# A hybrid retention/SSD layer on eight cores: x's third chunk moved ahead of two weight slabs, a norm weight folded into w_out, fewer LayerNorm statistics, more work on GpSimd, warm-up matmuls, and a new instruction order

## The chip, the cores and the metric

The kernel runs on all 8 cores of one Trainium2 chip. Each core works on its own requests with the same weights. There is no traffic between cores. The time of a run is that of its slowest core, in device microseconds.

Engines: PE is TensorE (matmul), DVE is VectorE, ACT is ScalarE, POOL is GpSimd, SP is the engine that issues part of the DMAs.

## The reference, cut to what matters

```python
def adaln(cond, w_ada, b_ada):
    return jax.nn.silu(cond) @ w_ada + b_ada            # 12 slabs of w_ada in the kernel

def trunk_layer(x, mod, rope, s_ret0, s_ssd0, p):
    sh1, sc1, g1, sh2, sc2, g2 = jnp.split(mod, 6, axis=-1)
    h = x * (1 + sc1) + sh1
    proj = h @ p['w_in']                                # q k v g (retention, 4 heads), z x B C dt (SSD)
    ...                                                 # bidirectional retention and SSD scans
    o_ssd = rms_norm(y * silu(z)) * p['ssd_norm_w']
    mix = jnp.concatenate([o_ret, o_ssd], axis=-1) @ p['w_out']
    x = layer_norm(ALPHA * x + g1 * mix, p['ln1_g'], p['ln1_b'])
    h2 = x * (1 + sc2) + sh2
    ffn = (silu(h2 @ p['w_gate']) * (h2 @ p['w_up'])) @ p['w_down']
    return layer_norm(ALPHA * x + g2 * ffn, p['ln2_g'], p['ln2_b']), ...
```

Per core there are 1536 tokens in three chunks of 512. Chunk 2 is context (group A). Chunks 0 and 1 are latent (group B).

## The kernel before

The kernel records operations and orders them itself when it is built: a list scheduler simulates the engines with a cost table and fixes one instruction order for each engine. Each engine then runs its list strictly in that order. Loads have an assumed duration in that table:

```python
            if o.is_dma:
                s0 = max(srv[0], st + 1.3)
                srv[0] = s0 + o.nbytes / (290e3 if e == POOL else 320e3)
                o.fin = srv[0] + 1.2          # the same for every core
# ... emit:
        self.schedule({})                     # first order, to learn lifetimes
        ...
            extra = self.place(slack)         # SBUF addresses; reuse gives extra dependencies
        order = self.schedule(extra)          # final order
```

Priorities (a lower level goes first), the order of stages and the triggers of loads are parameters. An entry such as `xr1="b2"` lets the rows of x for group A be fetched when the projections of latent head 2 are done.

```python
LV = dict(ht=0.9, conv=1.1, tm=1.1, prep=1, ssdA=0.8, ssdB=1, ..., headA=2, headB=1.7, evA=0.9, evB=0, outA=1.6,
          outB=1.5, evoA=0.7, evoB=0, ada=1.2)
SEQ = ("ssdA", "headA", "ssdB", "ada", "headB", "outA", "outB")
LD = dict(..., a6="p0A", a8="z7", h13="a1", a7="b0", a9="b0", ..., xr1="b2", xr0="b3", gate01="a3", ...)
```

A slab of weights is 128 x 4096 float32 in HBM and lands as bfloat16, by a DMA from the POOL queue. The start, and three places that the change touches:

```python
    w_in[1] = slab_load("w_in1", w_in_d[1], 4096, after=[xTo[(2, 1)]])
    ada[0] = slab_load("ada0", w_ada_d[0], 4096, after=[xTo[(2, 1)]])   # shift vector, first half
    ada[1] = slab_load("ada1", w_ada_d[1], 4096, after=[xTo[(2, 1)]])
    for q in range(2):                                                  # x, third chunk
        xTo[(1, q)] = P.dma(POOL, xT[(1, q)], xT_d[1, :, ...], after=[xTo[(2, 1)]])
    # ...
    def ssd_prep(g):                       # dt, decay: a chain of small ops on DVE and ACT
        ts(UU, AX, 1.0, ALU.add); act(LL, UU, AF.Ln); ...; tt(AX, AX, LL, ALU.mult); ...
    # ... end of ssd_block: norm weight applied while PSUM is evicted
        tt(oT[t // 4][:, :, o_:o_ + 128], ps..., nwc..., ALU.mult)
    # ... LayerNorm after the out-projection
        tt(dst[:, hs], bank, gate[:, hs], ALU.mult)
        stt(dst[:, hs], xres[:, hs], ALPHA, dst[:, hs], ALU.mult, ALU.add, accum_out=col(s, 16 * i))
        act(junk[:, hs], dst[:, hs], AF.Square, accum_out=col(s, 16 * i + 8))
```

## Time and profile before

| | before |
|---|---|
| time, median of 4 runs | 736.64 us (735.62 to 737.09) |
| span of the profiled slowest core | 733.4 us |
| PE busy / DVE / ACT / POOL | 91 / 56 / 42 / 32% |
| start of the block of 1516 matmuls (FFN and down projection) that nothing interrupts | 403.41 us |

From the page of the profile, before: the span, the busy times, and the two rows that show PE and its granted clock in 40 equal slices of the span (tenths).

```profile
span 733.4 us, 13130 instructions; the slowest of 8 cores (722.6 to 733.4 us)
PE 664.6 (91%) x4186; PEld 346.7 (47%) x4186; DVE 411.7 (56%) x896; ACT 309.1 (42%) x546; POOL 236.9 (32%) x277
PE   0598999999969989945999999999999999999995
PEclk9898999999999999976999999999999999999998
```

PE is idle in the first slices and dips around slices 18 and 19, where its clock falls too. From about 348 us on it is full. The longest waits of PE on this core (who waited for whom, us in total, times, longest):

```profile
PE psum L632 <- ACT arena L657: 22.5, 7, 16.2
PE psum L632 <- DVE arena L690: 11.1, 1, 11.1
PE psum L632 <- DMA arena<-w_ada: 5.7, 2, 4.9
PE psum L632 <- DMA arena<-w_in: 1.6, 1, 1.6
```

The first is mostly the start, which the change keeps. The 11.1 us wait is the seam: LayerNorm A is late and the FFN cannot begin. The same core by stretches: window, its length, then busy us (and instructions) of PE, PE weight load, DVE, ACT and POOL, then granted clock, DMA share and GB/s.

```profile
55.00:110.00 55.00, 51.44 (x460) 31.66 (x459) 30.56 (x90) 45.91 (x72) 17.55 (x56) 0.94 0.85 170
110.00:165.00 55.00, 53.95 (x359) 28.72 (x357) 43.04 (x82) 46.64 (x76) 36.20 (x45) 1.00 0.30 68
165.00:257.00 92.00, 82.24 (x711) 49.15 (x710) 75.15 (x123) 49.04 (x79) 49.18 (x56) 0.98 0.67 120
257.00:348.00 91.00, 69.35 (x600) 45.27 (x598) 68.58 (x139) 47.89 (x78) 51.45 (x50) 0.87 0.54 111
```

Window minus PE busy is PE's idle time: 3.6, 1.1, 9.8 and 21.7 us.

### The profile page before, as it was taken

The numbers are of one execution on the slowest core, as the hardware profiler recorded it, in microseconds if no ns is written. First come the engines' busy times: TensorE is split into PE (matmuls) and PEld (weight loads), VectorE is DVE, ScalarE is ACT, GpSimd is POOL, SyncE is SP. The second block draws the span as 40 slices with busy tenths as digits, with TensorE's granted clock in tenths as the row PEclk, the third lists the DMA queues.
The fourth block names the chain that finished last, engine by engine and source line by source line (L and its number), as shares of the span: only waits on it lengthen the run. The fifth ranks groups of instructions, "written<-read, shape, count | busy, mean of one in ns | idle before, by whom it ended". The sixth has DMA issues, their size and how long they took to land.

```text
span 733.4 us, 13130 instructions; the slowest of 8 cores (722.6 to 733.4 us)
## 1 busy us (share of the span) xinstructions
PE 664.6 (91%) x4186; PEld 346.7 (47%) x4186; DVE 411.7 (56%) x896; ACT 309.1 (42%) x546; POOL 236.9 (32%) x277
## 2 busy tenths in 40 slices
PE   0598999999969989945999999999999999999995
PEld 0255654556544656624446444444444444444443
DVE  5746275899867968877687212122112112486666
ACT  2657898877662445537556211111111111222221
POOL 3104042896454567543120169940000000000000
PEclk9898999999999999976999999999999999999998
DMA  8999951068982489430135433326292002022111
GB/s 249 332 171 240 173 96 46 21 137 151 161 153 52 87 138 177 126 109 1 58 102 130 115 57 58 59 44 124 49 171 44 1 30 86 1 87 87 57 58 58
DMA packets 14643, 75.08 MB, mean 102 GB/s; under 512 B 2656, under 2 KB 3040, under 8 KB 7920
## 3 DMA queue, kind: packets, MB, share of 16 engines
q0 software_dynamic: 5616, 42.47, 32.3%
q1 hardware_dynamic: 8960, 31.77, 12.9%
q8 instruction: 35, 0.57, 0.3%
q14 instruction: 32, 0.26, 0.1%
HBM read 106.05 MB, written 8.40 MB: 156 GB/s over the span
## 4 chain that ended last, share of the span: by engine, by line
PE 78%; DMA 10%; issue 4%; DVE 4%; ACT 2%; POOL 2%; SPq 1%; DVEq 0%; ACTq 0%; POOLq 0%
PE psum L632 76%; DMA arena<-w_in 5%; DMA arena<-w_ada 4%; DVE arena L682 2%; PE psum L635 2%; DVE arena L696 1%; POOL arena L682 1%; ACT arena L657 1%; ACT L657 1%; SPq L192 1%; DVE arena L690 0%; POOL arena L192 0%; POOL arena L707 0%; DVE arena L717 0%; DVE arena L720 0%
## 5 line engine op out<-in xcount | busy, mean ns | idle before, releaser
L632 PE MATMUL psum<-arena 128*128 128x512 bf16 (+5 forms) x4078 | 652.7, 319 | 60.5 <-ACT arena L657 22.5
L632 PEld LDWEIGHTS psum<-arena 128*128 128x128 bf16 x4078 | 333.6, 99 | 374.8 <-issue 86.9
L682 POOL TENSOR_TENSOR arena<-arena 128x512 f32<-128x512 f32 (+5 forms) x160 | 197.1, 1249 | 138.9 <-ACT arena L657 39.2
L657 ACT ACTIVATE arena<-psum 128x512 bf16<-128x512 f32 (+2 forms) x184 | 104.6, 579 | 243.1 <-PE psum L632 209.9
L682 DVE TENSOR_TENSOR arena<-arena,psum 128x512 bf16<-128x512 bf16 (+3 forms) x134 | 86.7, 653 | 180.9 <-PE psum L632 175.9
L657 ACT ACTIVATE arena<-arena 128x512 bf16<-128x512 f32 (+7 forms) x200 | 113.5, 588 | 145.4 <-DVE arena L696 92.7
L682 DVE TENSOR_TENSOR arena<-psum,arena 128x512 f32<-128x512 f32 (+6 forms) x187 | 116.6, 643 | 42.7 <-PE psum L632 37.1
L696 DVE SCALAR_TENSOR_TENSOR arena<-arena 128x512 f32<-128x512 f32 (+1 forms) x99 | 71.0, 752 | 4.3 <-DVE arena L682 2.3
L657 ACT ACT_TABLE_LOAD x43 | 55.2, 1283 | 19.2 <-PE psum L632 9.7
L657 ACT ACTIVATE arena<-psum,arena 128x512 bf16<-128x512 f32 (+2 forms) x58 | 36.1, 648 | 12.2 <-PE psum L632 6.9
L690 DVE TENSOR_SCALAR arena<-arena 128x1 f32<-128x1 f32 (+2 forms) x112 | 23.1, 216 | 31.1 <-ACT arena L657 21.6
L707 DVE CAST arena<-psum 128x512 bf16<-128x512 f32 (+2 forms) x42 | 25.2, 605 | 14.3 <-PE psum L632 10.7
L682 DVE TENSOR_TENSOR arena<-arena 128x8 f32<-128x8 f32 (+8 forms) x55 | 22.3, 412 | 4.6 <-PE psum L632 3.2
L707 POOL CAST arena<-arena 128x2 bf16<-128x2 f32 (+1 forms) x51 | 13.0, 345 | 31.3 <-DVE arena L707 24.8
L707 DVE CAST arena<-arena 128x256 bf16<-128x256 f32 (+8 forms) x35 | 17.4, 500 | 8.6 <-DMA arena<-w_ada 5.1
L192 POOL DMA_DIRECT2D arena<-w_gu x11 | 6.3, 572 | 49.4 <-PE psum L632 28.6
L1289 DVE COPY_PREDICATED psum<-arena,psum 128x512 f32<-128x512 uint16 x24 | 16.6, 693 | 9.8 <-PE psum L632 9.5
L688 DVE TENSOR_SCALAR arena<-arena 128x128 bf16<-128x128 f32 (+5 forms) x78 | 17.1, 266 | 6.0 <-ACT arena L657 5.4
L635 PE MATMUL psum<-arena 128*128 128x128 f32 (+1 forms) x108 | 15.7, 291 | 0.8 <-DVE arena L717 0.6
L192 POOL DMA_DIRECT2D arena<-w_in x10 | 6.0, 604 | 29.8 <-DVE arena L688 26.1
L635 PEld LDWEIGHTS psum<-arena 128*128 128x128 f32 (+1 forms) x108 | 13.5, 150 | 4.2 <-issue 2.7
L720 DVE TENSOR_SCALAR arena<-arena 128x512 bf16<-128x512 f32 x24 | 11.4, 511 | 4.1 <-DMA arena<-xT 4.0
(20 smaller groups left out, 58.7 us busy)
## 6 DMA issues: line engine op xcount, KB each, us to landing
arena<-w_gu POOLq DMA_DIRECT2D x11, 1024.0 KB, 10.1
arena<-w_in POOLq DMA_DIRECT2D x10, 1024.0 KB, 13.5
arena<-w_ada POOLq DMA_DIRECT2D x10, 1024.0 KB, 17.5
arena<-x SPq DMA_DIRECT2D x12, 512.0 KB, 3.5
arena<-w_down POOLq DMA_DIRECT2D x4, 1408.0 KB, 16.5
y<-arena SPq DMA_DIRECT2D x11, 512.0 KB, 2.7
arena<-w_ada SPq DMA_DIRECT2D x4, 1024.0 KB, 15.8
arena<-xT SPq DMA_DIRECT2D x4, 1024.0 KB, 22.1
```

The source lines that it names most:

```text
L192: o = self.add({eng: (0.9 if eng == POOL else 0.45, lambda e: e.dma_start(out=R(out), in_=R(in_)))}, [in_], [out], after=after)
L632: return P.add({PE: (c, lambda e: e.matmul(R(out), lhsT=R(lhsT), rhs=R(rhs), start=start, stop=stop))}, [lhsT, rhs], [out])
L635: return P.add({PE: (0.12, lambda e: e.transpose(out=R(out), in_=R(in_), identity=R(ident_f)))}, [in_, ident_f], [out])
L657: fn = lambda e: e.activation(out=R(out), in_=R(in_), func=func, **{k: R(v) for k, v in kw.items()})
L682: fn = lambda e: e.tensor_tensor(out=R(out), in0=R(in0), in1=R(in1), op=op)
L688: fn = lambda e: e.tensor_scalar(out=R(out), in0=R(in0), scalar1=R(s1), scalar2=None, op0=op0)
L690: fn = lambda e: e.tensor_scalar(out=R(out), in0=R(in0), scalar1=R(s1), scalar2=R(s2), op0=op0, op1=op1)
L696: fn = lambda e: e.scalar_tensor_tensor(out=R(out), in0=R(in0), scalar=R(scalar), in1=R(in1), op0=op0, op1=op1, **{k: R(v) for k, v in kw. ...
L707: alts[g] = (vcost(g, out, [in_], "copy"), lambda e: e.tensor_copy(out=R(out), in_=R(in_)))
L720: lambda e: e.tensor_scalar(out=R(out), in0=R(in_), scalar1=R(scale), scalar2=R(bias), op0=ALU.mult, op1=ALU.add))
L1289: P.add({DVE: (0.7, lambda e, eb=eb, ef=ef, mk_=mk_: e.copy_predicated(R(eb), R(mk_), R(ef)))}, [mk_, ef, eb], [eb])
```

## The change

Intent: fill PE's idle stretches and take small work off DVE. The diff, cut to its core:

```diff
+WARM = 8
-LV = dict(ht=0.9, conv=1.1, tm=1.1, prep=1, ssdA=0.8, ssdB=1, ... evA=0.9, evB=0, outA=1.6, outB=1.5, evoA=0.7, evoB=0, ada=1.2)
+LV = dict(ht=1.1, conv=1.1, tm=1, prep=1.1, ssdA=0.8, ssdB=0.8, ... evA=0, evB=0, outA=1.6, outB=1.5, evoA=1.25, wo=1.2, evoB=0.7, ada=1.7)
-OPT = dict(rope="q")
+OPT = dict(rope="qk", swap="")                # k's rotary swap by ACT and POOL too
+ENG = dict(wo="V", pr="P", ht="AVP", ...)     # SSD prep on POOL; modulation of x on ACT, DVE or POOL
-SEQ = ("ssdA", "headA", "ssdB", "ada", "headB", "outA", "outB")
+SEQ = ("ssdA", "headA", "ada", "ssdB", "outA", "headB", "outB")
-LD = dict(... a7="b0", a9="b0", ... xr1="b2", ...)
+LD = dict(... a7="b2", a9="a3", ... xr1="b1", ...)
 ...                                           # ring sizes and the SBUF placement search also changed
-    ada[0] = slab_load("ada0", ...)
-    ada[1] = slab_load("ada1", ...)
     for q in range(2):
         xTo[(1, q)] = P.dma(POOL, xT[(1, q)], ...)
+    for half in range(2):
+        ada[half] = slab_load("ada%d" % half, ...)
 ...
+    for i in range(WARM):                      # result unused
+        P.add({PE: (0.22, lambda e: e.matmul(R(idle), lhsT=R(ident_b), rhs=R(ident_b4), ...))}, ..., after=[xTo[(2, 1)]])
 ...
-        ts(UU, AX, 1.0, ALU.add)
+        ts(UU, AX, 1.0, ALU.add, eng=EN["pr"])             # and some 15 more like it per group
 ...
-        tt(oT[t // 4][...], ps..., nwc..., ALU.mult)
+        cp(oT[t // 4][...], ps..., (ACT, DVE))
 ...
+        for k in range(4):
+            ts(wo[half][:, 4 + k, :], wo[half][:, 4 + k, :], nwc[:, k:k + 1], ALU.mult, eng=EN["wo"])
 ...
-    ts(pq, col(s, 8), 1.0 / 1024.0, ALU.mult, EPS, ALU.add)  # one small op fewer per LayerNorm: the Square is scaled instead
```

More of the change, by code (lines that the diff above doesn't have):

```diff
@@ L131, in __init__ @@
         self.ops, self.bufs, self.level, self.tag = [], [], 1, ""
-        self.pools, self.reserve, self.margin, self.turns = {}, {}, 0.0, 16
+        self.pools, self.reserve, self.margin, self.turns = {}, {}, 0.0, 20
     def buf(self, name, n, dt=F32):
@@ L414, in place, with fill @@
         best = None
-        boost = {}
         keys = [lambda x: (-x[2].nbytes * (x[1] - x[0] + 20), x[0]), lambda x: (-(x[1] - x[0]), x[0]),
                 lambda x: (x[0], -x[2].nbytes), lambda x: (-x[2].nbytes, x[0])]
-        for turn in range(4 + self.turns):
-            if turn < 4:
-                src = sorted(live, key=keys[turn])
-            else:
-                if best[0] <= ARENA:
-                    break
-                src = sorted(base, key=lambda x: -boost.get(x[2], 0))
+        def fill(src, cut):
             placed, top = [], 0
@@ L427, in place @@
                 ov = sorted((q[3], q[3] + q[2].nbytes) for q in placed if q[0] < t1 + slack and t0 < q[1] + slack)
-                cur = 0
-                for a_, e_ in ov:
-                    if a_ - cur >= b.nbytes:
-                        break
-                    cur = max(cur, e_)
+                if b.nbytes >= cut:
+                    cur = 0
+                    for a_, e_ in ov:
+                        if a_ - cur >= b.nbytes:
+                            break
+                        cur = max(cur, e_)
+                else:
+                    hi, cur = ARENA, None
+                    ends = sorted(ov, key=lambda q: -q[1])
+                    for a_, e_ in ends:
+                        if hi - e_ >= b.nbytes:
+                            break
+                        hi = min(hi, a_)
+                    cur = hi - b.nbytes
+                    if cur < 0:
+                        cur = max([e_ for a_, e_ in ov] + [ARENA])
@@ L433, in place @@
                 placed.append((t0, t1, b, cur))
                 top = max(top, cur + b.nbytes)
-            if best is None or top < best[0]:
-                best = (top, placed)
-                base = src
-            over = [q[2] for q in placed if q[3] + q[2].nbytes > ARENA]
-            if turn == 3:
-                base = [q[:3] for q in best[1]]
-                over = [q[2] for q in best[1] if q[3] + q[2].nbytes > ARENA]
-            if turn >= 3:
-                for b in over:
-                    boost[b] = boost.get(b, 0) + 1
-                base = src if turn > 3 else base
+            return top, placed
@@ new lines, in place @@
+        for cut in (0, 4096):
+            boost, base = {}, None
+            loc = None
+            for turn in range(4 + self.turns):
+                if loc is not None and loc[0] <= ARENA:
+                    break
+                src = sorted(live, key=keys[turn]) if turn < 4 else sorted(base, key=lambda x: -boost.get(x[2], 0))
+                top, placed = fill(src, cut)
+                if loc is None or top < loc[0]:
+                    loc, base = (top, placed), src
+                if turn >= 3:
+                    for q in (loc[1] if turn == 3 else placed):
+                        if q[3] + q[2].nbytes > ARENA:
+                            boost[q[2]] = boost.get(q[2], 0) + 1
+                    if turn > 3:
+                        base = src
+            if best is None or loc[0] < best[0]:
+                best = loc
+            if best[0] <= ARENA:
+                break
@@ L562 @@
 EARLY_CK = (2, 0)
+WARM = 8
 MARGIN = 0.0
 NSEL = 3
-LV = dict(ht=0.9, conv=1.1, tm=1.1, prep=1, ssdA=0.8, ssdB=1, ssdi=0, retA=1.1, retB=1.1, reti=0.1, headA=2, headB=1.7, evA=0.9, evB=0, outA=1.6,
-          outB=1.5, evoA=0.7, evoB=0, ada=1.2)
-OPT = dict(rope="q")
-ENG = dict(dg="V", wg="V", y2="VP", xw="P", sd="P", zm="P", qf="VP", rg="P", ra="P", rd="VP")
-SEQ = ("ssdA", "headA", "ssdB", "ada", "headB", "outA", "outB")
-RING = dict(W=2, P=2, y1=3, y2=2, yb=3, xw=2, Sd=2, Sf=3, Sfb=3, hB=2, hA=4, vs=1, kt=3, PT=1, sq=2, rg=2, qf=3, rp=2, xr=2)
-LD = dict(w2="w0", h10="p1B", h11="p1B", a4="p1B", a5="p1A", h12="z7", a6="p0A", a8="z7", h13="a1", a7="b0", a9="b0", wo0="z11", wo1="a1", h00="a2",
-          h01="a3", a10="a0", a11="a3", h02="oA", h03="b1", rope="z3", S0f="oA", xr1="b2", xr0="b3", gate01="a3", gate00="b2", ln1="f0", g0="b1", g1="oA",
-          g2="f0", g3="b0", g4="oB", g5="oB", g6="f4", g7="f3", g8="f6", g9="f1", g10="f2", wd0="f5", wd1="f4", wd2="f6", wd3="f6", ln2="f10", gate11="f9",
+LV = dict(ht=1.1, conv=1.1, tm=1, prep=1.1, ssdA=0.8, ssdB=0.8, ssdi=0, retA=1.1, retB=1.3, reti=0, headA=2, headB=1.7, evA=0, evB=0, outA=1.6,
+          outB=1.5, evoA=1.25, wo=1.2, evoB=0.7, ada=1.7)
+OPT = dict(rope="qk", swap="")
+ENG = dict(wo="V", pr="P", ht="AVP", sm="V", dg="V", wg="V", y2="P", xw="P", sd="P", zm="P", qf="VP", rg="P", ra="P", rd="VP")
+SEQ = ("ssdA", "headA", "ada", "ssdB", "outA", "headB", "outB")
+RING = dict(W=3, P=2, y1=2, y2=2, yb=1, xw=2, Sd=1, Sf=3, Sfb=2, hB=3, hA=3, vs=1, kt=1, PT=2, sq=1, rg=3, qf=4, rp=2, xr=2)
+LD = dict(w2="w0", h10="p1C", h11="p1A", a4="p1B", a5="p0B", h12="z11", a6="p0A", a8="b0", h13="a0", a7="b2", a9="a3", wo0="z3", wo1="a1", h00="a2",
+          h01="a3", a10="z11", a11="a1", h02="oA", h03="b1", rope="z3", S0f="a3", xr1="b1", xr0="b3", gate01="a3", gate00="b1", ln1="f0", g0="b1", g1="a3",
+          g2="b2", g3="oA", g4="oB", g5="oB", g6="f4", g7="f1", g8="f1", g9="f0", g10="f1", wd0="f8", wd1="f7", wd2="f9", wd3="f8", ln2="f10", gate11="f9",
           gate10="f10")
@@ L697, in stt, with cp @@
         return P.add({g: (vcost(g, out, [in0, in1], "tt"), fn) for g in eng}, [in0, in1, scalar], [out] + list(kw.values()))
-    def cp(out, in_, eng=(DVE,)):
+    def cp(out, in_, eng=(DVE,), after=()):
         eng = eng if isinstance(eng, tuple) else (eng,)
@@ L707, in cp @@
                 alts[g] = (vcost(g, out, [in_], "copy"), lambda e: e.tensor_copy(out=R(out), in_=R(in_)))
-        return P.add(alts, reads, writes)
+        return P.add(alts, reads, writes, after=after)
     def affine(out, in_, scale, bias, eng=(ACT, DVE)):
         alts = {}
+        if POOL in eng:
+            alts[POOL] = (vcost(POOL, out, [in_], "ts"),
+                          lambda e: e.tensor_scalar(out=R(out), in0=R(in_), scalar1=R(scale), scalar2=R(bias), op0=ALU.mult, op1=ALU.add))
         if ACT in eng:
@@ L752, in build @@
     smalls = cols[:, C_SMALL:C_SMALL + 40]
+    ident_b4 = ident_b.unsqueeze(1).to_broadcast([128, 4, 128])
     tcol = P.buf("tcol", 4)
@@ L809, in build @@
     w_in[1] = slab_load("w_in1", w_in_d[1], 4096, after=[xTo[(2, 1)]])
-    ada[0] = slab_load("ada0", w_ada_d[0], 4096, after=[xTo[(2, 1)]])
-    ada[1] = slab_load("ada1", w_ada_d[1], 4096, after=[xTo[(2, 1)]])
     for q in range(2):
@@ L814, in build @@
         xTo[(1, q)] = P.dma(POOL, xT[(1, q)], xT_d[1, :, q * 2048:(q + 1) * 2048], after=[xTo[(2, 1)]])
+    for half in range(2):
+        ada[half] = slab_load("ada%d" % half, w_ada_d[half], 4096, after=[xTo[(2, 1)]])
     EV["w0"], EV["x0"], EV["x1"] = o_w0, xTo[(0, 1)], xTo[(1, 1)]
@@ L817, in build @@
     S0s = P.buf("S0s", 1024)
-    P.dma(SP, S0s, sssd_d[:, :], after=[xTo[(1, 1)]])
     scv = P.buf("scv", 16, BF16)
@@ L882, in build @@
     P.level = 3
-    for i in range(NSEL):
-        cp(selx[i][0:96, :].rearrange("p (r t) -> p r t", r=16), cols[0:96, C_SEL:C_SEL + 16].unsqueeze(2).to_broadcast([96, 16, 128]), POOL)
     delta = P.buf("delta", 384)
@@ L960, in make_hT @@
             q = kt // 4
-            affine(hT3[ck][:, kt, :], xT[(ck, q)][:, (kt % 4) * 512:(kt % 4) * 512 + 512], sc1p[q][:, kt % 4, c:c + 1], sh1[q][:, kt % 4, c:c + 1])
+            affine(hT3[ck][:, kt, :], xT[(ck, q)][:, (kt % 4) * 512:(kt % 4) * 512 + 512], sc1p[q][:, kt % 4, c:c + 1], sh1[q][:, kt % 4, c:c + 1], EN["ht"])
+    P.level = 0
+    idle = P.ps("mod", early=True).rearrange("p (a b) -> p a b", a=4)
+    for i in range(WARM):
+        P.add({PE: (0.22, lambda e: e.matmul(R(idle), lhsT=R(ident_b), rhs=R(ident_b4), start=True, stop=True))}, [ident_b], [idle], after=[xTo[(2, 1)]])
     LV_EV, LV_MIX, LV_DENSE, LV_BG = 0, 1, 2, 3
@@ L1052, in build @@
     w_in[2] = slab_load("w_in2", w_in_d[2], 4096, ev="w2")
+    P.dma(SP, S0s, sssd_d[:, :], after=[ada[1][1]])
+    P.level = 3
+    for i in range(NSEL):
+        cp(selx[i][0:96, :].rearrange("p (r t) -> p r t", r=16), cols[0:96, C_SEL:C_SEL + 16].unsqueeze(2).to_broadcast([96, 16, 128]), POOL, [ada[1][1]])
     proj(0, 1)
@@ L1154, in ssd_prep @@
         act(AX, AX, AF.Exp, scale=-1.0)
-        ts(UU, AX, 1.0, ALU.add)
+        ts(UU, AX, 1.0, ALU.add, eng=EN["pr"])
         act(LL, UU, AF.Ln)
-        ts(UU, UU, -1.0, ALU.add, 1e-30, ALU.max)
+        ts(UU, UU, -1.0, ALU.add, 1e-30, ALU.max, eng=EN["pr"])
         recip(UU)
-        tt(LL, LL, UU, ALU.mult)
-        tt(AX, AX, LL, ALU.mult)
-        ts(X, X, 0.0, ALU.max)
-        tt(DT, X, AX, ALU.add)
-        ts(DT, DT, 1e-30, ALU.max)
-        tt(LA, DT, nA.unsqueeze(1).to_broadcast([128, nb, 16]), ALU.mult)
+        tt(LL, LL, UU, ALU.mult, eng=EN["pr"])
+        tt(AX, AX, LL, ALU.mult, eng=EN["pr"])
+        ts(X, X, 0.0, ALU.max, eng=EN["pr"])
+        tt(DT, X, AX, ALU.add, eng=EN["pr"])
+        ts(DT, DT, 1e-30, ALU.max, eng=EN["pr"])
+        tt(LA, DT, nA.unsqueeze(1).to_broadcast([128, nb, 16]), ALU.mult, eng=EN["pr"])
         act(LNDT, DT, AF.Ln)
@@ L1172, in ssd_prep @@
         cp(RS[:, :, 0:8], CUM[:, :, 0:8])
-        tt(RS[:, :, 8:16], LA[:, :, 8:16], CUM[:, :, 8:16], ALU.subtract)
-        tt(RS[:, :, 16:24], LNDT[:, :, 0:8], CUM[:, :, 0:8], ALU.subtract)
-        tt(RS[:, :, 24:32], LNDT[:, :, 8:16], RS[:, :, 8:16], ALU.subtract)
+        tt(RS[:, :, 8:16], LA[:, :, 8:16], CUM[:, :, 8:16], ALU.subtract, eng=EN["pr"])
+        tt(RS[:, :, 16:24], LNDT[:, :, 0:8], CUM[:, :, 0:8], ALU.subtract, eng=EN["pr"])
+        tt(RS[:, :, 24:32], LNDT[:, :, 8:16], RS[:, :, 8:16], ALU.subtract, eng=EN["pr"])
         cp(EXPIN[:, :, 0:8], RS[:, :, 0:8])
-        tt(EXPIN[:, :, 8:16], TOT[:, :, 8:16], RS[:, :, 8:16], ALU.add)
-        tt(EXPIN[:, :, 16:24], TOT[:, :, 0:8], RS[:, :, 16:24], ALU.add)
+        tt(EXPIN[:, :, 8:16], TOT[:, :, 8:16], RS[:, :, 8:16], ALU.add, eng=EN["pr"])
+        tt(EXPIN[:, :, 16:24], TOT[:, :, 0:8], RS[:, :, 16:24], ALU.add, eng=EN["pr"])
         cp(EXPIN[:, :, 24:32], RS[:, :, 24:32])
@@ L1183, in ssd_prep @@
         cp(SPL[:, :, 0:32], H1)
-        tt(R1, RS, SPL[:, :, 0:32], ALU.subtract)
+        tt(R1, RS, SPL[:, :, 0:32], ALU.subtract, eng=EN["pr"])
         cp(H1, R1)
         cp(SPL[:, :, 32:64], H1)
-        tt(R1, R1, SPL[:, :, 32:64], ALU.subtract)
+        tt(R1, R1, SPL[:, :, 32:64], ALU.subtract, eng=EN["pr"])
         cp(H1, R1)
@@ L1327, in ssd_block @@
         o_ = (t % 4) * 128
-        tt(oT[t // 4][:, :, o_:o_ + 128], ps.rearrange("p (j t) -> p j t", j=4), nwc.unsqueeze(2).to_broadcast([128, 4, 128]), ALU.mult)
+        cp(oT[t // 4][:, :, o_:o_ + 128], ps.rearrange("p (j t) -> p j t", j=4), (ACT, DVE))
     P.level = LV_BG
@@ L1336, in build @@
     cos_t, sin_t = rope[:, 0:1024], rope[:, 1024:2048]
-    rtA, rtB = Ring("ropeA", RING["rp"], 512), Ring("ropeB", RING["rp"], 512)
+    rtA, rtB, rtC = Ring("ropeA", RING["rp"], 512), Ring("ropeB", RING["rp"], 512), Ring("ropeC", 1, 512)
     rk = {g: {n: Ring("%s_%d" % (n, g), (RING["hB"] if g == GB else RING["hA"]), 512 * len(CK[g]), BF16) for n in ("q", "k", "v", "g")} for g in (GA, GB)}
@@ L1400, in head @@
                     tt(tA, ps, cos_t[:, tsl], ALU.mult)
-                    if name in OPT["rope"]:
+                    if name in OPT["swap"]:
+                        tC = rtC()
+                        cp(tC, ps, (ACT, DVE))
+                        P.dma(SP, tB[0:64, :], tC[64:128, :])
+                        P.dma(SP, tB[64:128, :], tC[0:64, :])
+                        tt(tB, tB, sin_t[:, tsl], ALU.mult, EN["ra"])
+                    elif name in OPT["rope"]:
                         cp(tB[0:64, :], ps[64:128, :], (ACT,))
@@ L1477, in wo_load @@
         wo[half] = slab_load("wo%d" % half, w_out_d[half], 4096, ev="wo%d" % half)[0].rearrange("p (k n) -> p k n", k=8)
+        P.level = LV["wo"]
+        for k in range(4):
+            ts(wo[half][:, 4 + k, :], wo[half][:, 4 + k, :], nwc[:, k:k + 1], ALU.mult, eng=EN["wo"])
     ln2 = P.buf("ln2", 2048)
@@ L1480, in build @@
     rst = Ring("lnst", 6, 88)
-    S_SMALL, S_MEAN, S_MSQ, S_NVAR, S_LN, S_RSTD, S_B = 48, 56, 57, 64, 72, 73, 80
+    S_SMALL, S_MEAN, S_MSQ, S_POS, S_VAR, S_LN, S_RSTD, S_B = 48, 56, 57, 58, 64, 72, 73, 80
     H = (slice(0, 512), slice(512, 1024))
@@ L1499, in piece, with moments @@
         stt(dst[:, hs], xres[:, hs], ALPHA, dst[:, hs], ALU.mult, ALU.add, accum_out=col(s, 16 * i))
-        act(junk[:, hs], dst[:, hs], AF.Square, accum_out=col(s, 16 * i + 8))
-    def moments(s, n):
-        pm, pq = col(s, 0), col(s, S_SMALL)
-        ts(pq, col(s, 8), 1.0 / 1024.0, ALU.mult, EPS, ALU.add)
+        act(junk[:, hs], dst[:, hs], AF.Square, scale=1.0 / 32.0, accum_out=col(s, 16 * i + 8))
+    def moments(s, n, sign):
+        pm, pq = col(s, 0), col(s, 8)
         for i in range(1, n - 1):
-            q_, m_ = col(s, S_SMALL + 2 * i), col(s, S_SMALL + 2 * i + 1)
-            ts(q_, col(s, 16 * i + 8), 1.0 / 1024.0, ALU.mult, pq, ALU.add)
+            m_, q_ = col(s, S_SMALL + 2 * i), col(s, S_SMALL + 2 * i + 1)
             ts(m_, col(s, 16 * i), pm, ALU.add)
+            ts(q_, col(s, 16 * i + 8), pq, ALU.add)
             pm, pq = m_, q_
         i = n - 1
-        ts(col(s, S_MEAN), col(s, 16 * i), pm, ALU.add, 1.0 / 1024.0, ALU.mult)
-        ts(col(s, S_MSQ), col(s, 16 * i + 8), 1.0 / 1024.0, ALU.mult, pq, ALU.add)
-        ts(col(s, S_NVAR), col(s, S_MEAN), col(s, S_MEAN), ALU.mult, col(s, S_MSQ), ALU.subtract)
+        ts(col(s, S_MEAN), col(s, 16 * i), pm, ALU.add, -1.0 / 1024.0, ALU.mult)
+        ts(col(s, S_MSQ), col(s, 16 * i + 8), pq, ALU.add, EPS, ALU.add)
+        if sign < 0:
+            ts(col(s, S_VAR), col(s, S_MEAN), col(s, S_MEAN), ALU.mult, col(s, S_MSQ), ALU.subtract)
+        else:
+            ts(col(s, S_POS), col(s, 16 * i), pm, ALU.add, 1.0 / 1024.0, ALU.mult)
+            ts(col(s, S_VAR), col(s, S_POS), col(s, S_MEAN), ALU.mult, col(s, S_MSQ), ALU.add)
     h2T, aT = {}, {}
@@ L1538, in out_stage @@
                 piece(x1[t], banks[half], xr, gate, H[half], s, half, junk)
-            moments(s, 2)
-            ts(col(s, S_MSQ), col(s, S_NVAR), -1.0, ALU.mult)
-            tt(col(s, S_RSTD), col(s, S_MSQ), mhalf[:, 0:1], ALU.pow, POOL)
-            ts(col(s, S_B), col(s, S_MEAN), col(s, S_RSTD), ALU.mult, -1.0, ALU.mult)
+            moments(s, 2, 1)
+            tt(col(s, S_RSTD), col(s, S_VAR), mhalf[:, 0:1], ALU.pow, POOL)
+            ts(col(s, S_B), col(s, S_MEAN), col(s, S_RSTD), ALU.mult)
             for half in range(2):
@@ L1600, in down @@
                     s = st_[t]
-                    moments(s, 1 + parts)
-                    act(col(s, S_LN), col(s, S_NVAR), AF.Ln, scale=-1.0)
+                    moments(s, 1 + parts, -1)
+                    act(col(s, S_LN), col(s, S_VAR), AF.Ln, scale=-1.0)
                     act(col(s, S_RSTD), col(s, S_LN), AF.Exp, scale=-0.5)
@@ L1607, in down @@
                     for hs in hss:
-                        stt(w[:, hs], u[t][:, hs], col(s, S_MEAN), ln2[:, hs], ALU.subtract, ALU.mult)
+                        stt(w[:, hs], u[t][:, hs], col(s, S_MEAN), ln2[:, hs], ALU.add, ALU.mult)
                     for hs in hss:
```

## The prediction

> **What bounds it now.** The page of the slowest core (span 733.4 us): PE busy 664.6 us (91%), DVE 56%, ACT 42%, POOL 32%; the chain of waits puts 76% on one matmul line. Only PE's 69 us of idle time and its low-clock stretches can shrink. The table of stretches and the PE waits place them:
>
> - 0 to 36.6 us: 25 idle. The chain waits for the last half of w_in until 35.4, behind some 9 MB at about 300 GB/s. The change keeps this.
> - 63.7 to 68: 3.3 idle, for the shift vector from w_ada halves 0 and 1; PE has nothing else, as xT's third chunk queues behind those slabs.
> - 165 to 220: 8 idle, of which 5.7 on w_ada and 1.6 on w_in (cores 0 and 2: 4 less).
> - 312 to 348: 18.7 idle, granted clock 0.71 and 0.63. The context out-projection's LayerNorm starts only at about 305, so its transposes (340 to 346) and the FFN behind them wait; one wait is 11.1 us.
> - Tail: 6. From 348 on PE is saturated; nothing there changes.
>
> Low clock costs about 6 us more in 312 to 348 (17.3 busy at 0.67), and a few us in 37 to 110: matmuls start every 425 ns just after 36.6, against 213 later. The Trainium skill, "TensorE: Matmul & The Clock Gate", Part 1, says an idle PE falls to half rate and needs about 3.4 us of activity to recover; these spacings agree.
>
> **What the change does.**
> 1. Third x chunk first: projections of chunk 1 (64 matmuls, 14 us) cover the wait for w_ada: -3 us.
> 2. Eight warm-up matmuls, about 3.4 us cold, fit the idle stretch before 36.6: -1.
> 3. Context out-projection before the latent heads, its x rows one head earlier: LayerNorm A runs while heads still feed PE. Of 24 us (18.7 idle + 6 clock) I expect 12 back (0 to 20). The main term.
> 4. w_ada stage earlier, other triggers: -3, uncertain in sign.
> 5. DVE relief: SSD prep (some 30 ops of 0.2 to 0.3 us) to POOL, k's rotary swap (8 pairs of 0.69) to ACT and POOL, the norm-weight product (12 x 0.69) becomes a plain copy on ACT or DVE, against 8 multiplies on w_out rows. DVE is off the bound. "SBUF — State Buffer", "two separate sides", calls the DVE/GpSimd port pair an exclusive lock; at 306 to 311 a 0.68 us DVE op took 1.75 beside POOL work. More POOL work risks more of these: +2.
> 6. One small DVE op fewer per LayerNorm (about 0.2 us): -0.2 at the tail.
> 7. New stalls from reordered loads and tighter rings: +2 to +3.
>
> Sum: about -17 us.
>
> **Predicted: 719 us, 709 to 731.** Faster by over 2%: 0.57; within 2%: 0.41; slower: 0.02.
>
> **What would show it.** PE idle near 64 gone (1); first matmuls after 36 at 213 ns (2); no 11 us wait at the seam into the FFN, clock near 1 there, FFN begins about 15 us earlier (3); less PE wait on w_ada (4); DVE busy down 15 to 25 us, POOL up 15 to 30 (5). FFN and down unchanged at about 0.216 us per matmul.
>
> **What would make it wrong.** The idle time moves instead of vanishing: POOL-bound rotary or prep chains, loads gated on later events, or memory placement forcing false waits; then it stays above 725. If the seam fills completely and the w_ada waits go too, it comes under 710.

## More of the kernel before

The spans of all cores:

```profile
core 0: 724.7 us, clock 0.971
core 1: 733.4 us, clock 0.969
core 2: 722.6 us, clock 0.975
core 3: 731.8 us, clock 0.969
core 4: 731.0 us, clock 0.977
core 5: 723.5 us, clock 0.975
core 6: 729.9 us, clock 0.975
core 7: 727.4 us, clock 0.971
```

Take the cores in neighbouring pairs (0 and 1, 2 and 3, and so on): in each pair one is longer.

## The result, and the profile after

| | before | after |
|---|---|---|
| time, median of 4 runs | 736.64 us | 728.89 us (727.33 to 731.32) |
| ratio, 95% interval | | 0.990 (0.987 to 0.993) |
| repeated later, 5 rounds on another chip | 736.79 us | 729.65 us, ratio 0.9912 (0.9895 to 0.9928) |

A ratio is the mean time of one kernel's runs over that of the other's of the same rounds, so it is not quite the ratio of the medians quoted. Executions in which one die ran at a lower clock are left out of the means. The time lies inside the predicted range, but the gain is 7 us where the sum said 17. The page of after, its slowest core:

```profile
span 728.3 us, 13074 instructions; the slowest of 8 cores (710.6 to 728.3 us)
PE 666.4 (91%) x4194; PEld 347.2 (48%) x4194; DVE 393.8 (54%) x824; ACT 312.6 (43%) x561; POOL 263.4 (36%) x322
PE   0799999989896998787999999999999999999995
PEclk9899999999998999999999999999999999999998
```

The deep dip at slices 18 and 19 has turned into several shallow ones from slice 8 on. The waits of PE that answer to those of before:

```profile
PE psum L650 <- ACT arena L675: 20.7, 8, 12.8
PE psum L650 <- DVE arena L725: 7.7, 2, 4.8
PE psum L650 <- DMA arena<-w_ada: 7.0, 2, 4.8
PE psum L650 <- DMA arena<-w_in: 1.8, 1, 1.8
PE psum L650 <- DVE psum L1318: 2.1, 1, 2.1
```

The single wait of 11.1 us is gone. Of the 7.7 us for DVE L725, 4.8 belong to the start and 2.9 to the time around 299 us. The waits for w_ada and w_in did not shrink: 8.8 us against 7.3. By stretches:

```profile
55.00:110.00 55.00, 54.83 (x525) 33.28 (x523) 32.47 (x81) 43.28 (x74) 32.14 (x89) 0.99 0.71 123
110.00:165.00 55.00, 51.80 (x337) 27.68 (x337) 38.30 (x58) 40.55 (x66) 39.45 (x47) 0.97 0.61 117
165.00:257.00 92.00, 82.17 (x714) 49.49 (x712) 74.66 (x120) 60.62 (x95) 59.27 (x65) 0.96 0.60 116
257.00:348.00 91.00, 73.85 (x622) 47.83 (x620) 62.77 (x124) 53.81 (x92) 58.92 (x56) 0.96 0.52 111
```

PE's idle time is now 0.2, 3.2, 9.8 and 17.2 us. The first stretch gained 3.4, the second lost 2.1, the third gained nothing, the last gained 4.5. The block of 1516 matmuls starts at 397.50 us instead of 403.41 and lasts 322.56 us in both. Now all cores:

```profile
core 0: 724.2 us, clock 0.977
core 1: 713.9 us, clock 0.984
core 2: 713.1 us, clock 0.984
core 3: 726.9 us, clock 0.980
core 4: 728.3 us, clock 0.976
core 5: 713.8 us, clock 0.983
core 6: 727.3 us, clock 0.976
core 7: 710.6 us, clock 0.982
```

Four cores finish near 713, four near 727, one of each kind in every pair. In the repeated rounds, on cores 0 to 3, the longer core of a pair went from 734.2 to 727.8 us on average (-6.4) and the shorter from 724.7 to 713.9 (-10.8). Which core of a pair is the longer one changes from run to run, so it is no property of a core's data. The pair gap is there before the FFN begins; the FFN block itself lasts 322.56 us on every core. The change gained 11 us where it does not count and 6 where it does.

One thing that differs inside a pair is when loads land. The issues of the two cores at the same point of the program (core 4, long, at 207 us; core 5, short, at 201 us), KB as they land, and us from issue to landing:

```profile
arena<-w_ada POOLq DMA_DIRECT2D x1, 1024.0 KB, 15.6
```

```profile
arena<-w_ada POOLq DMA_DIRECT2D x1, 1024.0 KB, 11.5
```

And the waits of PE for w_ada between 165 and 257 us on these two cores, core 4 first:

```profile
PE psum L650 <- DMA arena<-w_ada: 7.0, 2, 4.8
```

```profile
PE psum L650 <- DMA arena<-w_ada: 0.7, 1, 0.7
```

The Trainium skill, "HBM Reference", Specifications, says that the two cores of a pair share one memory's bandwidth. The pairs of long and short cores agree with that. No run here left a core's neighbour idle, so the sharing itself is not shown. These waits are one part of the gap. Between cores 4 and 5 it is 14.5 us; PE's idle time differs by 6.2 us from 165 to 257 us and by another 4.9 from 257 to 348, where e14 below finds a second cause.

What became of the main term, the LayerNorm of the context, can be read from DVE's timeline. These are the first and the last addition of an x row before that LayerNorm, first in before (core 1), then in after (core 4), as start, us, engine, line and op:

```profile
306.23 1.75 DVE L696 SCALAR_TENSOR_TENSOR arena<-arena 128x512 f32<-128x512 f32 x1
319.28 1.09 DVE L696 SCALAR_TENSOR_TENSOR arena<-arena 128x512 f32<-128x512 f32 x1
```

```profile
288.80 1.48 DVE L714 SCALAR_TENSOR_TENSOR arena<-arena 128x512 f32<-128x512 f32 x1
317.50 1.62 DVE L714 SCALAR_TENSOR_TENSOR arena<-arena 128x512 f32<-128x512 f32 x1
```

It starts 17.4 us earlier, but its last row comes only 1.8 us earlier. The kernels' instruction lists, built again, show one likely reason: the 64 matmuls of the context out-projection stand among those of the latent heads in both kernels (places 1533 to 1652 of PE's list before, 1716 to 1883 after; the heads end at 2283 and 2263). They were not moved ahead of the heads. DVE's list of waits shows another: core 4 waits once, 4.6 us, for x rows, and in before none of cores 0 to 3 does.

### The profile page after: what moved, and what is told of

It reads as the page before. It is cut to its first block, busy times and chain, and to the rows that moved or that the text cites. A ratio compares the mean times of both kernels' runs of the same rounds, so it can differ in the third digit from the quotient of the medians.

```text
span 728.3 us, 13074 instructions; the slowest of 8 cores (710.6 to 728.3 us)
## 1 busy us (share of the span) xinstructions
PE 666.4 (91%) x4194; PEld 347.2 (48%) x4194; DVE 393.8 (54%) x824; ACT 312.6 (43%) x561; POOL 263.4 (36%) x322
## 4 chain that ended last, share of the span: by engine, by line
PE 78%; DMA 10%; POOL 4%; issue 4%; DVE 2%; ACT 1%; SPq 1%; DVEq 0%; POOLq 0%; ACTq 0%
PE psum L650 76%; DMA arena<-w_in 4%; POOL arena L700 3%; DMA arena<-x 3%; DMA arena<-w_ada 2%; PE psum L653 2%; DMA ossd<-arena 1%; ACT arena L675 1%; DVE arena L700 1%; SPq L192 1%; DVE arena L714 0%; DVE arena L708 0%; DVE arena L741 0%; DVE psum L1318 0%; DVEq L553 0%
## 5 line engine op out<-in xcount | busy, mean ns | idle before, releaser
L700 POOL TENSOR_TENSOR arena<-arena 128x512 f32<-128x512 f32 (+8 forms) x193 | 216.8, 1143 | 104.9 <-DVE arena L708 30.6
L675 ACT ACTIVATE arena<-psum 128x512 bf16<-128x512 f32 (+3 forms) x201 | 115.3, 582 | 220.8 <-PE psum L650 207.8
L675 ACT ACTIVATE arena<-arena 128x512 bf16<-128x512 f32 (+6 forms) x203 | 113.4, 579 | 161.0 <-DVE arena L714 96.6
L700 DVE TENSOR_TENSOR arena<-psum,arena 128x512 f32<-128x512 f32 (+4 forms) x159 | 98.2, 635 | 65.1 <-PE psum L650 56.9
L725 DVE CAST arena<-psum 128x512 bf16<-128x512 f32 (+2 forms) x53 | 31.6, 607 | 20.9 <-PE psum L650 17.3
L192 POOL DMA_DIRECT2D arena<-w_down x4 | 2.1, 530 | 101.1 <-PE psum L650 101.1
L706 DVE TENSOR_SCALAR arena<-arena 128x128 bf16<-128x128 f32 (+6 forms) x81 | 21.4, 310 | 4.6 <-POOL arena L700 4.1
L708 DVE TENSOR_SCALAR arena<-arena 128x1 f32<-128x1 f32 (+1 forms) x85 | 18.6, 226 | 9.4 <-ACT arena L675 6.2
L725 DVE CAST arena<-arena 128x1024 bf16<-128x1024 f32 (+8 forms) x28 | 15.0, 549 | 9.8 <-DMA arena<-w_ada 6.9
L653 PE MATMUL psum<-arena 128*128 128x128 f32 (+1 forms) x108 | 15.6, 292 | 4.2 <-DVE arena L700 2.1
L1318 DVE COPY_PREDICATED psum<-arena,psum 128x512 f32<-128x512 uint16 x24 | 16.5, 691 | 4.5 <-PE psum L650 4.2
L192 POOL DMA_DIRECT2D arena<-w_ada x10 | 5.8, 585 | 30.9 <-PE psum L650 16.7
L741 DVE TENSOR_SCALAR arena<-arena 128x512 bf16<-128x512 f32 x23 | 13.3, 613 | 5.0 <-DMA arena<-xT 4.9
## 6 DMA issues: line engine op xcount, KB each, us to landing
arena<-w_down POOLq DMA_DIRECT2D x4, 1408.0 KB, 10.8
```

The costliest lines, as they stand in the source:

```text
L192: o = self.add({eng: (0.9 if eng == POOL else 0.45, lambda e: e.dma_start(out=R(out), in_=R(in_)))}, [in_], [out], after=after)
L653: return P.add({PE: (0.12, lambda e: e.transpose(out=R(out), in_=R(in_), identity=R(ident_f)))}, [in_, ident_f], [out])
L675: fn = lambda e: e.activation(out=R(out), in_=R(in_), func=func, **{k: R(v) for k, v in kw.items()})
L700: fn = lambda e: e.tensor_tensor(out=R(out), in0=R(in0), in1=R(in1), op=op)
L706: fn = lambda e: e.tensor_scalar(out=R(out), in0=R(in0), scalar1=R(s1), scalar2=None, op0=op0)
L708: fn = lambda e: e.tensor_scalar(out=R(out), in0=R(in0), scalar1=R(s1), scalar2=R(s2), op0=op0, op1=op1)
```

## The experiments

Theory T1: the new order does give about 11 us, but the core of each pair that is served later waits for late w_ada and w_in slabs, and it sets the time. Rival R1: loads are not what held the gain back; the seam and the GpSimd chains were simply worth less.

The experiments keep the SBUF placement of the kernel they edit, because the kernel after fills its part of SBUF to the last byte and most edits do not fit otherwise. "Same order" means that each engine's list is the same, checked by comparing the lists.

### e1 and e2: half the bytes, same order

```diff
-        o = P.dma(POOL, b, src, after=after)
+        if ev is not None and ev[0] in "ah":       # later w_ada slabs, head slabs of w_in
+            o = P.dma(POOL, b[:, 0:n // 2], src[:, 0:n // 2], after=after)
+            o.nbytes *= 2                          # the scheduler still sees a full slab
+        else:
+            o = P.dma(POOL, b, src, after=after)
 # and the matmuls on these slabs read wv[:, kt % 4, ...] in place of wv[:, kt, ...]: wrong on purpose
```

> The kernel after, every instruction in the same order on every engine, but the loads of the later modulation slabs and of the head slabs bring half their bytes (the result is wrong on purpose; the matmuls use the loaded half twice). Theory T1 (the slowest core pays for loads that land late, because of two neighbour cores one is always served slower): the waits of 2.2 and 4.8 us on w_ada and 1.8 us on w_in vanish, all cores come to about 711 to 714 us, the time to 713 to 718 us, and the two cores of a pair differ by under 5 us. Rival R1 (the loads are not what held the gain back; the seam and the POOL chains are): time stays at 726 to 730 us.

> The kernel before with the same halving (wrong on purpose). T1: it gains its own late-load waits of about 7 us, so 727 to 731 us, and the two halved kernels then differ by about 13 us, more than the 7.7 us between the whole ones. R1: no change in either, the difference stays near 8 us.

| | time | ratio to before | longer / shorter core of a pair, cores 0 to 3 |
|---|---|---|---|
| before (chip of e9) | 736.79 us | 1 | 734.2 / 724.7 |
| after (e9) | 729.65 us | 0.9912 | 727.8 / 713.9 |
| e2, before with half bytes | 727.13 us | 0.9889 (0.9874 to 0.9905) | 725.1 / 723.6 |
| e1, after with half bytes | 715.91 us | 0.9738 (0.9722 to 0.9755) | 713.9 / 710.5 |

Both results are wrong (relative error 1.2). T1 holds, R1 falls. With loads in time the two kernels differ by 727.13 - 715.91 = 11.2 us. Late loads cost before 0.0111 of its time (8.2 us) and after 0.9912 - 0.9738 = 0.0174 (12.8 us). So the change made lateness dearer by 4.6 us (an estimate from the three intervals is 2 us either way), and the pairs close up once the loads are short. Shorter loads also make way for the other loads beside them, so this is the cost of these loads and of what they delay.

That the new order is tighter is not shown. In the scheduler's own table, built again, PE's first use is planned within 1 us of the landing for 6 of the 11 w_ada and w_in slabs issued after 100 us in before, 5 of 12 in after, and 2 of 12 in e8 and e10 below.

### e13 and e14: which loads

The same edit for one kind of slab alone.

```diff
-        if ev is not None and ev[0] in "ah":
+        if ev is not None and ev[0] == "a":        # e13; "h" in e14
```

> The kernel after in its own order; of the loads halved in e1, only the later modulation slabs (wrong on purpose). The waits of 2.2 and 4.8 us on the slowest core stand on w_ada: if that lateness is the slabs' own, 719 to 722 us. If it is rather the queue of other loads in front of them: under 3 us of gain, 725 us or more.

> The same with only the head slabs of w_in halved (wrong on purpose). They are twice on the way with w_ada and with the x rows, so if it is the shared queue: 718 to 722 us; if only the slabs that PE is seen waiting for matter: 725 to 727 us (the 1.8 us wait and the x rows).

The chip of these rounds ran cores 4 to 7 at a granted clock of 0.93 to 0.97 in every run. Cores 0 to 3 were at 0.965 or more in most runs; only those runs are used. Medians of the longest of cores 0 to 3: before 733.0 us (6 runs), e13 720.5 (5), e14 720.1 (6). In their own undisturbed rounds after gave 728.2 and e1 714.5 on these cores. Halving either kind takes away about 8 us, halving both about 14. The expectations had given two rival forms, the slabs' own lateness or a shared queue. The traces of cores 0 to 3 show two places instead. In e13 PE's idle time from 165 to 257 us is 3.5 to 4.6 us on all four cores (in after 8.6 to 9.8 on the longer ones), while from 257 to 348 us it is still 13.3 to 15.1. In e14 it is the other way round: 10.3 and 10.5 us stay on the longer cores in the first stretch, and the second falls to 10.6 to 12.3 (16.1 and 16.3 on the longer cores of after). e14's core 2, one of its longer cores, still waits for w_ada as after did:

```profile
PE psum L650 <- DMA arena<-w_ada: 7.0, 2, 4.7
```

In e14 PE's own waits for w_in are gone (2.1 and 2.6 us on the longer cores of after), and DVE's waits for x rows are short (0 to 2.0 us on these cores, 3.5 to 7.3 in after): a head slab is on its way with these rows, as e5 shows below. So late w_ada slabs, and head slabs with the x rows beside them, are two separate costs of about 8 us, and together they nearly add up to the 14 of e1.

### e3: an order that expects late loads

```diff
+        self.slow = 6.0                            # after the placement, before the final order
         order = self.schedule(extra)
-                o.fin = srv[0] + 1.2
+                o.fin = srv[0] + 1.2 + (self.slow if st > 100.0 and o.nbytes > 1e6 else 0.0)
```

> The kernel after with its memory placement kept, but the final order made with loads issued after 100 us counted as landing 6 us later; only the order of instructions changes. T1: PE no longer stands in front of a late slab, so the slow core of each pair gains 5 to 9 us: 719 to 724 us, spread within a pair under 8 us. R1: no gain, 727 us or more.

725.62 us, ratio 0.9886 (0.9855 to 0.9917). PE's list of waits has no w_ada and no w_in in it any more, and the pairs differ by 2 to 7 us. But the gain on after is only about 3 us, less than expected: the shorter cores became slower (717.3 us on average on cores 0 to 3, against 713.9), since the new order opens other gaps.

### e4: without the warm-up

```diff
-WARM = 8
+WARM = 0
```

> The kernel after without its eight warm-up matmuls, all else in the same order. The step was predicted to be worth 1 us (0 to 2). If right: 729 to 731 us. If the warm-up does nothing: 728 to 729 us; if it costs: below 728 us.

728.83 us, ratio 0.991 (0.9891 to 0.9929), like after. This rests on 3 runs of e4; a fourth, of 806.86 us, was slow. The eight matmuls are worth nothing that these runs can see. In after's trace they run from 30.48 us on for 3.57 us, PE then stands for another 2.5 us, and the first 19 matmuls from 36.72 us still take 5.68 us, about 0.30 us each against 0.213 warm. On cores 1, 3 and 6 the pause after the burst was 0.45 to 1.04 us and the first matmuls came every 0.21 to 0.22 us; the time did not profit.

### e5: x rows one head later

```diff
+        for o, ev in self.late_x:                  # the loads of x rows for group A, ev = latent head 2 done
+            o.deps.add(ev)
         order = self.schedule(extra)
```

> The kernel after, placement kept, but the rows of x for the context LayerNorm may be fetched only after latent head 2 (as in the kernel before), not head 1; the order follows. The prediction's main term said that this earlier trigger is what lets LayerNorm A run while heads still feed PE. If so, the seam before the FFN opens again and the time rises by 5 to 10 us, to 734 to 739 us. If the seam was closed by the new order alone: within 2 us of 729.

731.71 us, ratio 0.9959 (0.9938 to 0.9981): about 3 us slower than after, not 5 to 10. The prediction did not divide its main term of 12 us; this piece of it is worth about a quarter. In after these rows are no quick load either. The chain of waits of after has this piece (start, length, what):

```profile
275.92 20.58 DMA arena<-x
```

The first two rows are issued at 275.3 and 275.9 us, 23 us earlier than in before (298.3), but take 13.4 and 20.6 us to land, where before took at most 4.1. The new trigger also starts a slab of w_in at 275.9 us (19.8 us to landing) and one of w_gu at 276.5 (28.8).

### e6: SSD prep on DVE again

```diff
         order = self.schedule(extra)
+        move = {... 30 small ops on X, AX, UU, LL, DT, LA, RS, EXPIN, R1 ...}
+        # they go from POOL's list to DVE's, at the same start times; all other lists as they were
```

> The kernel after with 30 of the small SSD-prep ops on DVE again, at the same points in time, all other instructions in the same order. The prediction charged 2 us for more GpSimd work (slower small ops, waits for the shared SBUF ports). If that is real and on the path: 1 to 3 us faster, 726 to 728 us. If the move to GpSimd was worth something: slower, over 730. Neutral: 728 to 730.

726.31 us, ratio 0.9885 (0.9865 to 0.9904), 2 us under after's 0.9912 but with overlapping intervals. e10 below repeats it on another base. The two profiles show the ops themselves, first before (DVE), then after (POOL), as line, engine, op, shapes and count, then busy us and mean ns, then idle before:

```profile
L682 DVE TENSOR_TENSOR arena<-arena 128x64 f32<-128x64 f32 x10 | 2.2, 222 | 0.8 <-DVE arena L682 0.3
L682 DVE TENSOR_TENSOR arena<-arena 128x128 f32<-128x128 f32 x7 | 2.1, 297 | 0.1
```

```profile
L700 POOL TENSOR_TENSOR arena<-arena 128x64 f32<-128x64 f32 x9 | 2.9, 323 | 0.5
L700 POOL TENSOR_TENSOR arena<-arena 128x128 f32<-128x128 f32 x6 | 2.7, 456 | 0.8 <-DVE arena L752 0.3 <-DVE arena L725 0.2 <-PE psum L650 0.2
```

Two-input ops of the same shape take 1.45 and 1.54 times as long on POOL. Each group mixes additions, subtractions and products, and the counts differ by one. The Trainium skill, "GPSIMD Engine Reference", Performance versus the Vector engine, states 1.96 times for a large add; the direction agrees. There is a second way in which POOL costs DVE. From after's timeline of DVE and of POOL (start, us, engine, line, op):

```profile
144.61 3.43 DVE L725 CAST arena<-arena 128x512 bf16<-128x512 f32 x1
```

```profile
144.18 3.58 POOL L700 TENSOR_TENSOR arena<-arena 128x1 f32<-128x1 f32 x4
```

A cast that took 0.42 us at 125.17 us on this core took 3.43 while four one-column POOL ops ran, and the 2.1 us wait of PE for DVE L1318, shown above, is the op right behind it. The skill's "SBUF — State Buffer", "two separate sides", describes an exclusive lock that one instruction holds from its start to its end. The trace agrees with that only in part: the cast outlasted all four POOL ops, of about 0.9 us each, so one such hold does not explain it. No experiment separated it from other causes. These four ops are not the SSD prep, so e6 does not test this stall.

### e7, e8: the context out-projection first

In both the matmuls of the context out-projection get a level 0.4 lower. e7 also counts loads as 2 us late.

```diff
+        for o in self.ops:
+            if o.tag == "out1" and PE in o.alts:
+                o.key = (o.key[0] - 0.4, o.key[1])
+        self.slow = 2.0                            # e7; 0.0 in e8
         order = self.schedule(extra)
```

> The kernel after, placement kept, final order made with (a) loads after 100 us counted as landing 2 us later and (b) the matmuls of the context out-projection ranked ahead of the head projections. Theory: late loads and the starved seam are what is left, so both together give 6 to 9 us over after: 720 to 723 us, with a pair spread under 10 us. Otherwise 727 or more.

> Only (b) of e7. The seam gets 2 to 3 us shorter on every core but the late loads stay: 725 to 727 us, pair spread still 12 us or more.

e7: 731.86 us, ratio 0.9961 (0.9943 to 0.9979), slower than after and a clear miss. It hardly waits for loads (0.2 us on w_in, nothing on w_ada), but its order leaves about 8 us of PE idle between 165 and 257 us on all cores. e8: 723.36 us, ratio 0.9843 (0.9823 to 0.9863), better than expected. Its pairs differ by 4 to 11 us where 12 was expected. The two differ only in the assumed landing time.

### e9 to e12: after again, and combinations

e9 is after, unedited; its numbers stand in the tables above. Its ratio came as expected; the two cores of a pair differed by 4 to 19 us, mostly 14 to 15, where at least 12 was expected.

> The kernel after, unedited, so that small differences are judged on one chip in the same rounds. Ratio to before 0.990 again, about 728 us, one core of each pair 12 us or more longer than the other.

e10 is e8's level change plus e6's move. e11 is e8's level change with only the modulation slabs counted as 4 us late. e12 is e11 with e6's move.

> e8's ranking of the context out-projection and e6's SSD prep on DVE together. If the GpSimd prep really costs 1 to 2 us on the path: 721 to 722.5 us, that is 5 to 7 us under after of the same rounds. If e6's gain was noise: as e8, 723 to 724 us.

> e8's ranking, and the final order made with only the later modulation slabs counted as landing 4 us later. If PE's standing in front of w_ada is what the slow core of each pair still pays: 719 to 722 us and a pair spread under 9 us. If the new order only opens other gaps, as in e7: 724 us or more.

> e11 with the SSD prep on DVE. Best case of the study if all three add up: 718 to 721 us, ratio to before 0.977 to 0.982; if they do not add up: as the better of e10 and e11.

| | time | ratio to before (5 rounds) |
|---|---|---|
| e9, after | 729.65 us | 0.9912 (0.9895 to 0.9928) |
| e10 | 721.85 us | 0.9800 (0.9785 to 0.9815) |
| e11 | 726.69 us | 0.9860 (0.9843 to 0.9877) |
| e12 | 727.01 us | 0.9872 (0.9855 to 0.9889) |

e10 is correct and the fastest kernel that is: 7.8 us under after, 14.9 under before. Next to e8 (0.9843) it shows the prep on DVE as worth about 3 us. e11 and e12 missed. Planning for later loads gave something once in e3 and cost something in e7 and e11: a single assumed delay is no cure, and small changes of it shift the whole order. So a gain of 2 or 3 us by one of these reorderings is partly luck of the order, and e12 shows that the prep's gain depends on the order too.

### e15: e10 with half the bytes

> e10 (context out-projection ranked first, SSD prep on DVE) with e1's halving (wrong on purpose). If the terms are independent, e10's 7.8 us come off e1's 716: 708 to 711 us. If e10's gain was itself a better cover for late loads: 712 to 715 us.

e1's edit on e10, in the rounds with the disturbed die. Longest of cores 0 to 3: 714.0 us (6 runs), against e1's 714.5 in its own rounds. With loads in time the longer cores of e10 and after are alike (the shorter ones averaged 708.2 against 710.5, on different chips). So most of the 7.8 us that e10 gained is a better cover for late loads. The terms are not independent, as the prediction's sum took them to be.

### e16: the stall of step 1, by shorter loads

```diff
-    ada[0] = slab_load("ada0", w_ada_d[0], ...); ada[1] = slab_load("ada1", ...)
+    for half in range(2):                          # kernel before, same order, wrong on purpose
+        b = P.buf("ada%d" % half, 4096, BF16)
+        ada[half] = (b, P.dma(POOL, b[:, 0:1024], w_ada_d[half, :, 0:1024], after=[xTo[(2, 1)]]))
```

> The kernel before in its own order, with w_ada halves 0 and 1 bringing a quarter of their bytes (wrong on purpose), so that the shift vector and x's third chunk both arrive about 10 us sooner. This takes away the wait that step 1 was to cover. Step 1 was sized at 3 us: 731 to 733 us. If the restart at low clock after that wait also counts: 729 to 731 us.

Longest of cores 0 to 3: 733.05 us (4 undisturbed runs) against 733.0 for before. Nothing came of it. The waits of PE between 60 and 75 us on core 0 of e16:

```profile
PE psum L632 <- POOL arena L707: 2.1, 1, 2.1
PE psum L632 <- DVE arena L682: 1.3, 1, 1.3
```

The stall is there as before, without any DMA in it. It is a chain: small matmuls, a DVE add, small matmuls, POOL casts, then the convolution, in a fixed order with nothing between. The prediction had called it a wait for the slabs. In after it is gone, and PE has the projections of chunk 1 to do meanwhile.

## Why the prediction was right or wrong

The time lies inside the range because the range is wide. The prediction thought a gain of over 2% likelier than not, and the gain was 1.0%. It had also named what happened as a way to be wrong, "The idle time moves instead of vanishing", with a time above 725 us, but had given it too little weight.

Right:

- What cannot change: FFN and down took 322.56 us in both. The first 37 us hardly moved.
- Step 1, -3 us: idle from 55 to 110 us fell by 3.4. The mechanism (other work for PE) held; the cause read into it (late slabs) was wrong, as e16 shows.
- Step 5's counters: DVE busy fell by 17.9 us (15 to 25 foretold), POOL rose by 26.5 (15 to 30). Its cost, +2, fits e6 (2 us) and e10 against e8 (3 us); e12 against e11 shows none, so it depends on the order.

Right in size by luck:

- Step 7, "New stalls from reordered loads and tighter rings: +2 to +3". There are 2.1 us of new idle time from 110 to 165 us, but they are PE's wait behind the cast that ran slowly beside POOL ops (e6). That is nearer to what step 5 charged than to late loads or tight rings.

Wrong, by the terms of the sum of -17:

- Step 3, "Of 24 us (18.7 idle + 6 clock) I expect 12 back". This step failed, and it was the main term. The 11.1 us wait did vanish, but the idle time came back in small pieces: from 257 to 348 us the slowest core is idle 17.2 us instead of 21.7, a gain of 4.5; core 5, with 12.3 instead of 20.3, gained 8. The clock there rose from 0.87 to 0.96. The FFN block began 5.9 us earlier, not 15. What failed is the overlap that the step names, "LayerNorm A runs while heads still feed PE": the out-projection was not moved ahead of the heads in PE's list, the earlier x rows took 13.4 and 20.6 us to land instead of at most 4.1, and the LayerNorm's last row came 1.8 us earlier although its first came 17.4 us earlier. Halving the head slabs, some of which travel with the x rows, gave 8 us (e14).
- Step 4, "w_ada stage earlier, other triggers: -3, uncertain in sign". This step failed too. PE's idle time from 165 to 257 us stayed at 9.8 us, and the waits for w_ada and w_in on the slowest core went from 7.3 to 8.8 us: nothing in place of -3. The prediction noticed that cores 0 and 2 waited 4 us less, and did not ask why. The time is that of the late core of each pair. Late loads altogether cost 12.8 us instead of 8.2 (e1, e2): 4.6 more, which the sum did not contain. By e14 part of that belongs to the x rows of step 3; how it divides is not shown.
- Step 2, -1: nothing (e4).
- Step 6, -0.2 at the tail: nothing visible. From the end of the last matmul to the end of the last DVE op it was 5.28 us before (core 0) and 5.27 after (core 4).

The listed terms add up to about -15 us, not to the -17 that the prediction gives; that slip is 2 us of the miss. With loads in time the change is worth 11.2 us, about three quarters of 15. Late loads take 4.6 of these 11.2 away again. What stays open: whether the pairs come from the shared memory alone, and how the 11.2 us divide exactly, since the order changes as a whole and terms are not additive (e15).

## What to carry to other kernels

Look at all cores, not at the slowest alone: when spans fall into two groups, a change can gain 11 us on one and 6 on the other, and only the second counts. When you issue a load earlier, look at what is issued beside it: here the x rows started 23 us earlier and then took up to 20.6 us instead of at most 4.1. In a fixed order the engine that stands in front of a late load waits for it (7.0 us on core 4, 0.7 on its neighbour), whatever else is ready. When one long wait disappears, add up the short ones before you book the gain.

## What the Trainium skill lacked or had wrong

- "HBM Reference", Specifications: it gives an equal share per core of a pair. Here one core of each pair was served later, the same slab took 15.6 us on one and 11.5 on its neighbour, and the role changed between runs. The page does not mention an uneven split.
- "TensorE: Matmul & The Clock Gate", Part 1: the half rate after idling agrees (425 against 213 ns). A warm-up burst of 3.57 us followed by 2.5 us of idling bought nothing on core 4, whose granted clock is recorded as 0.5 from 29.2 to 39.5 us, through the burst and past it. Three cores with a pause of at most 1.04 us began warm, and the whole kernel's time was the same with the burst and without it (ratios 0.9912 and 0.991).
- "GPSIMD Engine Reference", Performance versus the Vector engine: it has the ratio at 2048 elements. At 64 and 128 elements two-input ops took 323 and 456 ns on POOL against 222 and 297 on DVE.
- "SBUF — State Buffer", "two separate sides": no figure for short ops. Four one-column POOL ops (3.58 us together) went with a cast of 3.43 us that took 0.42 elsewhere.
